# Norm steps in PSUM, four plain blocks at layer 1's second gated half, and three reorderings in a two-layer decoder trunk

## The chip, the cores and the metric

The kernel runs on one core of a Trainium2 chip. The metric is the device time of one execution in microseconds. The kernel before takes 2494.81 us, the median of three runs (2493.42 to 2498.12).

## What is computed

The reference runs a two-layer trunk over a prompt of 1024 tokens and 64 sample tokens (8 sequences of 8), with 1024 channels, in fp32. Every layer is a token mixer and a gated channel mixer, each with an RMS norm ahead and a residual add behind.

```python
def trunk(x, ...):
    h = x
    for layer in range(DEPTH):                       # 2
        hn = rms_norm(h, norm_mix_g[layer])
        if layer % 2 == 0:
            mix = conformer_sb_mixer(hn, ...)        # conv of width 31 | stick-breaking attention, paged cache
        else:
            mix = shortconv_pool_mixer(hn, ...)      # conv of width 3 | pooling of widths 2, 4, 8, 16
        h = h + mix
        h = h + swiglu(rms_norm(h, norm_ffn_g[layer]), w_ffn_in[layer], w_ffn_out[layer])
    return rms_norm(h, norm_final_g)

def rms_norm(x, g):
    return x * rsqrt(mean(x * x) + EPS) * g

def swiglu(h, w_in, w_out):                          # 1024 -> 2 x 2816 -> 1024
    g, u = split(h @ w_in, 2)
    return (silu(g) * u) @ w_out
```

For the sample tokens the keys and values of eight cache pages of 128 tokens per sequence are read through a page table. The outputs are the trunk's rows, the new keys and values and the new states.

## The kernel before

The 1088 tokens are two groups: GA, the first 512 tokens, and GB, the other 576 (512 of the prompt, 64 of the sample). Channels lie on the 128 partitions in eight tiles, tokens in the free dimension; `hb` holds the residual stream that way in SBUF.

Every fp32 product is three matmuls on fp32r operands: high by high, high by low, low by high. So each weight tile of 128x1024 (`stage`, loaded by SyncE's queue) is cut into a high part by ScalarE (L187, or L199 for halves) and a low part by GpSimd (L189, L200), into one of three tiles `hl`. Activations are cut the same way: a high copy on ScalarE, a low part (source minus high) on VectorE or GpSimd. The function `w_next` gives the next weight tile and lets the cuts of the tiles three ahead be issued.

A gated pair (one 128-column slice of gate and one of up) is made in one of two forms. The plain form (`one`) is two blocks of 8 x 3 matmuls over the group's token blocks. The other (`strassen`) takes seven products of half operands in place of eight: it needs sums of weight halves, which VectorE makes (L203 to L205, L217) and ScalarE and GpSimd cut, and sums of operand halves, which are made once per group (`sums_t`, L1743) and cut (`lows`, L1739). `PLAIN1` says how many of the 22 pairs of layer 1 are plain: none for GA, one for GB. A strassen pair of GB has 7 x 4 x 3 = 84 matmuls of 288 columns, a plain one 2 x 8 x 3 x 2 = 96.

A norm is made in these steps. The squares of the eight channel tiles are taken by ScalarE (L251, L254), and seven of the eight are added up into `ss` by GpSimd (L255). TensorE sums `ss` over the partitions, one matmul of one column for each 128 tokens (L262), into a PSUM tile `m`. ScalarE takes the square root (L267), and VectorE refines it in five small steps (L268 to L273), which pass through the SBUF tiles `nw` and `rstd`. VectorE then spreads the result on diagonals (L279), and TensorE (L288) and ScalarE (L289) bring it to `rr`, a row scale for all partitions.

The order of the work on each engine is the order in which the program issues it. The main flow is TensorE's matmuls, and at points between them, called slots, one piece of other work is issued: a step of a generator, or an entry of a list. The places that the change touches are these.

- The sample stage (`sample`, layer 0, beside GA's channel mixer): the attention of the sample tokens. Its last part multiplies weights with value pages, two pages of each of two sequences at a time (`pv`), as pages arrive; `pvq` holds these pieces.
- Layer 1's output of the mixer, GB's part: eight blocks. In their slots the generator `forms_a` makes GA's operands for the strassen products: the normed halves into `fa`, their sums into `fb`, the copies and the low parts. Behind each block `out_fin` adds to `hb` and issues the squares.
- Layer 1's channel mixer for GA (`channel1(GA, ...)`): 22 strassen pairs, with a piece of the output projection behind each pair from the third on. In its slots the generator `forms_b` makes GB's norm and its normed operands `xs`.
- The seam: behind the last pair `free_a` fills the list `seam`, which is worked off in the slots of the output's last pieces (`out_both`). It makes GB's plain operands `b1`, `b2` and, at the end, a part in a `hid` tile. Each of the four jobs of `jobs` makes sums of one quarter of `xs` and cuts them to the strassen operands in `xa`. Two jobs are part of `seam`; the other two are issued at every third slot of GB's plain pair.
- Then GB's channel mixer with the 22 pairs and the final norm.

Of the kernel before, what the change touches and what calls it, by code (L numbers as in the profile page):

```python
# [8 lines left out]
F = mybir.dt.float32  # L9
# [48 lines left out]
def trunk_kernel(ctx, tc, x_prompt, x_sample, cache_k, cache_v, state_conformer, state_shortconv, state_pool,  # L58
# [34 lines left out]
    rstd = consts.tile([128, 9], F, name="rstd")  # L93
    nw = consts.tile([128, 2, 9], F, name="nw")
    hb = hpool.tile([128, KC, T], F, name="hb")
# [43 lines left out]

    PLAIN, PLAIN1 = 5, (0, 1)  # L140

# [115 lines left out]

    def norm_cols(ps, count, t0, t1, more=None):
        m = ps()
        c = slice(t0, t1)  # L260
        for t in range(t0, t1):
            pe.matmul(m[:, t:t + 1], ss[:, t * 128:t * 128 + 128], ones[:, 0:1], start=True, stop=more is None)  # L262
            if more is not None:
                pe.matmul(m[:, t:t + 1], more[:, (t - t0) * 128:(t - t0) * 128 + 128], ones[:, 0:1], start=False,
                          stop=True)
        r = rstd[:, c]
        act.activation(r, m[:, c], AF.Sqrt, bias=eps, scale=1.0 / count)  # L267
        dve.tensor_scalar(nw[:, 0, c], m[:, c], 1.0 / count, EPS, op0=OP.mult, op1=OP.add)  # L268
        dve.reciprocal(r, r)

        dve.tensor_tensor(nw[:, 1, c], nw[:, 0, c], r, op=OP.mult)
        dve.scalar_tensor_tensor(nw[:, 1, c], nw[:, 1, c], -0.5, r, op0=OP.mult, op1=OP.mult)
        dve.scalar_tensor_tensor(r, nw[:, 1, c], 1.5, r, op0=OP.add, op1=OP.mult)  # L273

    def norm_a(g, ps, count, dg=None):
        norm_cols(ps, count, g.t0, g.t1)
        k = g.t1 - g.t0
        dg = tmp() if dg is None else dg
        dve.tensor_tensor(dg[:, :k * 128].rearrange("p (t n) -> p t n", t=k),  # L279
                          ident[:, None, :].to_broadcast([128, k, 128]),  # L280
                          rstd[:, g.t0:g.t1, None].to_broadcast([128, k, 128]), op=OP.mult)
        return dg
# [808 lines left out]
    def sample():  # L1091
# [5 lines left out]
        with ExitStack() as es_:  # L1097
# [192 lines left out]
            while s < len(steps) or chain or pvq or fins:  # L1290
# [6 lines left out]
                if s + 1 < len(steps):  # L1297
                    trans(*steps[s + 1], 0)
                if pvq and not soon and (s % 2 or s >= len(steps)):
                    pvq.pop(0)()  # L1300
                if todo and s < len(steps):
# [429 lines left out]
    def out_fin(g, n, a):  # L1731
        added(g, hb[:, n, g.cs], a)
        add_squares(g, hb[:, n, g.cs], n == 0)

# [16 lines left out]
    def forms_a(ep):  # L1751
        for _ in range(3):
            yield 1
        dg = norm_a(GA, ms, D, ep.tile([128, 1024], F, name="fa"))
        for _ in range(4):
            yield 1
        norm_b(GA, ms, dg)
        yield 1
        w = HALF // 2
        for k in range(4):  # L1760
            fa, fb = (ep.tile([128, 1024], F, name=n) for n in ("fa", "fb"))
            normed(fa[:, :HALF], k, GA.cs)
            normed(fa[:, HALF:], k + 4, GA.cs)
            dsts = ((b1[k][:, :, :w], fa[:, :w]), (b2[k][:, :, :HALF], fa[:, HALF:]),
                    (xa[k][:, :, :HALF], fb[:, :HALF]), (xa[4 + k][:, :, :HALF], fb[:, HALF:]))
            for o, i in dsts[:2]:
                act.activation(o[:, 0], i, AF.Copy)
            yield 1
            b11, b12, b21, b22, t2, t1, t4, t3 = (t[:, i * w:i * w + w] for t in (fa, fb) for i in range(4))
            sums_t(b11, b12, b21, b22, t1, t2, t3, t4)  # L1770
            for o, i in dsts[2:]:
                act.activation(o[:, 0], i, AF.Copy)
            for o, i in dsts[:2]:
                lows(o, i)
            yield 1
            for o, i in dsts[2:]:
                lows(o, i)
            yield 1
# [41 lines left out]


    def forms_b():
        dg = norm_a(GB, ms, D, xs[3])
        yield 1
        yield 1
        norm_b(GB, ms, dg)
        yield 1
        for k in range(4):
            normed(xs[k][:, 0:GB.n], k + 4, GB.cs)
            yield 1  # L1830
            normed(xs[k][:, GB.n:], k, GB.cs)
            yield 1
# [5 lines left out]
    def free_a():  # L1838
# [16 lines left out]
        def job(k):  # L1855
            low()
            b21, b22, b11, b12 = parts_b(k)
            fast = k < 2
            t3 = b12 if k > 1 else fp.tile([128, W2], F, name="t3", bufs=2)
            sums_t(b11, b12, b21, b22, b11, b22, t3, b21)  # L1860
            for o, x in ((xa[k], xs[k][:, W2:3 * W2]), (xa[4 + k][:, :, R], t3), (xa[4 + k][:, :, L], b21)):
                act.activation(o[:, 0], x, AF.Copy)
                if fast:
                    lowq.append(lambda o=o, x=x: lows(o, x))
                else:
                    lows(o, x)

        jobs.extend(lambda k=k: job(k) for k in range(4))
        seam.extend(jobs.pop(0) for _ in range(2))
        rest_b["f"] = last_part  # L1870
# [11 lines left out]
    def channel1(g, last, side, free, plain, x):  # L1882
# [4 lines left out]
        def slot():  # L1887
# [3 lines left out]
            if jobs and g is GB:  # L1891
                if turn[0] % 3 == 0:
                    jobs.pop(0)()
            elif turn[0] % 3 == 0:
                if g is GA or wj[0] > j0 + 2 * plain + 2:
                    next(side, 0)
# [48 lines left out]
    def to_y(hh):  # L1945
# [53 lines left out]
        def finish():  # L1999
            norm_cols(ms, D, 6, 9, last7)  # L2000
            for t in range(6, 9):
# [63 lines left out]
```

## Time and profile before

| | |
|---|---|
| median of three runs | 2494.81 us (2493.42 to 2498.12) |
| the profiled execution's own time | 2494.09 us |
| its span, first to last instruction | 2492.3 us |
| TensorE busy | 2415.4 us (97%) |
| VectorE, GpSimd, ScalarE busy | 1625.9, 1617.5, 1104.3 us |
| mean granted TensorE clock | 0.996 |

In the profile PE is TensorE, PEld its weight loads, DVE VectorE, ACT ScalarE, POOL GpSimd, and L262 line 262 of the kernel before. A row in order of time has the start and the length in us, the engine, line and operation, what is written from what, the shape and how many instructions were merged; in square brackets stand the idle time of the engine ahead of it and what ended that. A merged row's length reaches to the modelled end of its last matmul; the next row's start tells when TensorE went on. A row of the view of waits has the total, the number and the longest. A fp32 matmul that is not split stands as two instructions.

### The profile page before, as it was taken

The page shows a single profiled execution, that of the slowest core. Times are in us where ns is not written, and L with a number is a line of the kernel's source. Part 1 is how long each engine was busy: PE and PEld are TensorE (multiplying, and loading weights), DVE is VectorE, ACT ScalarE, POOL GpSimd, SP SyncE. Part 2 cuts the span into 40 slices and gives each one's busy share as a digit, 9 for nine tenths or more (in the row PEclk, how much of TensorE's full clock was granted, in tenths as well). Part 3 has the DMA queues.
Part 4 walks back from the last instruction along what each step waited for, and adds up shares of the span by engine and source line. Part 5 has one row for each costly group of instructions (what it writes and reads, how often), then busy time and mean ns, then how long its engine had stood idle before and what let it go on. Part 6 is the DMA issues. An engine that isn't in the chain of part 4 may idle for free.

```text
span 2492.3 us, 41476 instructions
## 1 busy us (share of the span) xinstructions
PE 2415.4 (97%) x15877; PEld 2188.2 (88%) x15877; DVE 1625.9 (65%) x2288; ACT 1104.3 (44%) x1877; POOL 1617.5 (65%) x1264
## 2 busy tenths in 40 slices
PE   8999999999999999999999999998999999999998
PEld 6788977788777679999999999888889988999998
DVE  3696878977777553766566533457666668666655
ACT  5535877754444343443333422234343344443333
POOL 6664344655554576787787523277888886887775
PEclk9999999999999999999999999999999999999999
DMA  7332241234665524223232311252333332233322
GB/s 224 113 109 75 76 123 43 72 111 137 179 181 169 161 90 152 77 69 100 87 98 85 113 52 43 61 150 62 92 102 102 100 96 85 85 102 113 92 85 81
DMA packets 355486, 258.32 MB, mean 104 GB/s; under 512 B 22913, under 2 KB 303617, under 8 KB 355272
## 3 DMA queue, kind: packets, MB, share of 16 engines
q1 hardware_dynamic: 355256, 255.66, 34.7%
q8 instruction: 126, 2.06, 0.3%
q14 instruction: 72, 0.59, 0.1%
q10 hardware_dynamic: 32, 0.01, 0.0%
HBM read 237.41 MB, written 18.69 MB: 103 GB/s over the span
## 4 chain that ended last, share of the span: by engine, by line
PE 75%; DVE 13%; POOL 5%; ACT 4%; issue 3%; DMA 1%; SPq 0%; DVEq 0%; ACTq 0%; POOLq 0%
PE acc L238 44%; PE acc L540 22%; POOL hl L200 2%; DVE q L1035 1%; DVE hb L300 1%; PE o L1057 1%; PE m L1159 1%; PE z L1182 1%; PE m L1047 1%; DVE cacc L858 1%; PE z L1018 1%; POOL hl L189 1%; DVE be L1037 1%; DVE sum L203 1%; DVE hid L244 1%
## 5 line engine op out<-in xcount | busy, mean ns | idle before, releaser
L189 POOL TENSOR_TENSOR hl<-stage,hl 128x512 fp32r<-128x512 f32 x464 | 638.6, 1400 | 391.6 <-ACT hl L187 279.9
L238 PE MATMUL acc<-x,hl 128*128 128x512 f32 (+1 forms) x3648 | 771.2, 349 | 11.3 <-DVE tmp L296 3.0
L238 PEld LDWEIGHTS acc<-x,hl 128*128 128x128 f32 x3648 | 585.6, 189 | 74.9 <-issue 5.8
L238 PE MATMUL acc<-hid,hl 128*128 128x288 f32 (+1 forms) x3096 | 542.1, 331 | 5.3 <-DVE hb L300 2.1
L238 PEld LDWEIGHTS acc<-hid,hl 128*128 128x128 f32 x3096 | 468.3, 189 | 51.0 <-DVE hb L300 4.2
L540 PE MATMUL acc<-x,hl 128*128 128x288 f32 (+1 forms) x2676 | 367.9, 291 | 7.9 <-POOL hl L200 3.7
L300 DVE TENSOR_TENSOR hb<-acc,hb 128x512 f32<-128x512 f32 (+1 forms) x360 | 255.5, 718 | 169.9 <-PE acc L238 168.6
L540 PEld LDWEIGHTS acc<-x,hl 128*128 128x128 f32 x2676 | 352.2, 189 | 14.1 <-POOL hl L200 7.0
L200 POOL TENSOR_TENSOR hl<-sum,hl 128x512 fp32r<-128x512 f32 x180 | 234.2, 1331 | 170.1 <-ACT hl L199 168.0
L187 ACT ACTIVATE hl<-stage 128x1024 fp32r<-128x1024 f32 x232 | 243.6, 1054 | 207.7 <-PE acc L238 141.4
L544 DVE TENSOR_TENSOR tmp<-acc,tmp 128x288 f32<-128x288 f32 (+1 forms) x420 | 174.4, 441 | 207.5 <-ACT tmp L556 102.1
L200 POOL TENSOR_TENSOR hl<-stage,hl 128x512 fp32r<-128x512 f32 x180 | 272.4, 1532 | 12.8 <-ACT hl L199 12.8
L540 PE MATMUL acc<-b,hl 128*128 128x256 f32 (+1 forms) x1548 | 216.0, 290 | 7.9 <-DVE tmp L544 5.8
L238 PE MATMUL acc<-x1t,hl 128*128 128x288 f32 x1152 | 216.3, 296 | 1.5 <-POOL hl L189 1.5
L540 PEld LDWEIGHTS acc<-b,hl 128*128 128x128 f32 x1548 | 201.7, 189 | 13.3 <-POOL hl L200 6.7
L238 PEld LDWEIGHTS acc<-x1t,hl 128*128 128x128 f32 x1152 | 195.9, 188 | 19.5 <-POOL hl L189 1.7
L199 ACT ACTIVATE hl<-sum 128x512 fp32r<-128x512 f32 x180 | 103.0, 623 | 187.5 <-DVE sum L205 164.6
L296 DVE TENSOR_TENSOR tmp<-acc,rr 128x512 f32<-128x512 f32 (+1 forms) x108 | 75.1, 710 | 128.1 <-PE acc L238 114.6
L199 ACT ACTIVATE hl<-stage 128x512 fp32r<-128x512 f32 x180 | 105.7, 619 | 70.4 <-PE acc L238 65.5
L507 POOL TENSOR_TENSOR tmp<-tmp 128x576 f32<-128x576 f32 (+1 forms) x85 | 124.3, 1462 | 9.2 <-ACT tmp L484 8.2
L238 PE MATMUL acc<-x1a,hl 128*128 128x512 f32 x480 | 122.6, 410 | 2.5 <-POOL hl L189 1.4
L255 POOL TENSOR_TENSOR ss<-ss,tmp 128x512 f32<-128x512 f32 (+1 forms) x69 | 106.3, 1541 | 25.9 <-ACT tmp L254 15.4
(299 smaller groups left out, 3129.6 us busy)
## 6 DMA issues: line engine op xcount, KB each, us to landing
stage<-in_w_ffn_in_dram SPq DMA_DIRECT2D x176, 512.0 KB
stage<-in_w_ffn_out_dram SPq DMA_DIRECT2D x88, 512.0 KB
stage<-in_w_in_even_dram SPq DMA_DIRECT2D x40, 512.0 KB
kst<-in_cache_k_dram SPq DMA_DIRECT2D x64, 256.0 KB
vst<-in_cache_v_dram SPq DMA_DIRECT2D x56, 256.0 KB
stage<-in_w_out_even_dram SPq DMA_DIRECT2D x16, 512.0 KB
stage<-in_w_in_odd_dram SPq DMA_DIRECT2D x16, 512.0 KB
stage<-in_w_out_odd_dram SPq DMA_DIRECT2D x16, 512.0 KB
```

The source lines that it names most:

```text
L187: act.activation(hl[:, 0], st, AF.Copy)
L189: pool.tensor_tensor(hl[:, 1, c], st[:, c], f32(hl[:, 0, c]), op=OP.subtract)
L199: act.activation(hl[:, 0, c], x, AF.Copy)
L200: pool.tensor_tensor(hl[:, 1, c], x, f32(hl[:, 0, c]), op=OP.subtract)
L203: todo = [lambda: dve.tensor_tensor(sb, su[:, lo], su[:, hi], op=OP.add), lambda: dve.tensor_tensor(sa[:, hi], sg[:, lo], su[:, lo], op=OP ...
L238: pe.matmul(acc[:, b, :c1 - c0], w, xs[:, xi, c0 - o:c1 - o], start=first and s == 0, stop=last and s == 2)
L255: pool.tensor_tensor(ss[:, g.cs], ss[:, g.cs], t[:, :g.n], op=OP.add)
L296: dve.tensor_tensor(d, a, r, op=OP.mult)
L300: dve.tensor_tensor(d, a, d, op=OP.add)
L507: (dve if both and f == NF - 1 else pool).tensor_tensor(t[:, :n], t[:, :n], u[:, :n], op=OP.mult)
L540: pe.matmul(acc[:, :w2], h[:, wi, i, k], xk[:, xi], start=k == 0 and s == 0, stop=k == 3 and s == 2)
L544: dve.tensor_tensor(out, acc[:, :w2], x, op=OP.add)
```

## The change

It has these parts.

1. The small norm steps no longer use `nw` in SBUF: they write other columns of the PSUM tile `m`, and where diagonals follow, the result stays there too.
2. For GB's norm in layer 1 the squares of channel tiles 4 to 7 are no longer added to `ss` by GpSimd. ScalarE writes them to the tiles `xs` (`square`), in the first four slots of GA's channel mixer, GpSimd clears 64 columns of each, and TensorE sums them with `ss`: five one-column matmuls for each 128 tokens. This norm is split into two pieces and stands later.
3. `forms_a` issues copies and low parts one slot behind the step that makes their source.
4. `PLAIN1` is (0, 2): pair 1 of GB is plain too. The first two jobs leave `seam`, and all four are issued at every third slot of the two plain pairs.
5. In the sample stage two slots pass ahead of the last `pv` piece.

At the start of GA's products GpSimd's order was, from the last weight tile of the mixer's output on (`ss` are the sums of squares, `hl` weight cuts; a number tells the pairs' sums apart):

```order
L189 TENSOR_TENSOR hl<-stage,hl 128x512 x2
L255 TENSOR_TENSOR ss<-ss,tmp 128x576
L200 TENSOR_TENSOR hl<-sum_17595,hl 128x512 x2
L255 TENSOR_TENSOR ss<-ss,tmp 128x576
L200 TENSOR_TENSOR hl<-sum_17596,hl 128x512
L200 TENSOR_TENSOR hl<-stage,hl 128x512
L255 TENSOR_TENSOR ss<-ss,tmp 128x576
L200 TENSOR_TENSOR hl<-stage,hl 128x512 x2
L255 TENSOR_TENSOR ss<-ss,tmp 128x576
L200 TENSOR_TENSOR hl<-sum_c,hl 128x512
```

and now it is:

```order
L188 TENSOR_TENSOR hl<-stage,hl 128x512 x2
L199 TENSOR_TENSOR hl<-sum_17589,hl 128x512 x2
L199 TENSOR_TENSOR hl<-sum_17590,hl 128x512
L199 TENSOR_TENSOR hl<-stage,hl 128x512 x3
L1836 MEMSET xs_17729 128x64
L199 TENSOR_TENSOR hl<-sum_c,hl 128x512
```

The four sums between the cuts are gone, and four small memsets have come in, of which the first is shown.

At the end of the sample stage TensorE's order was (`o` are the value products, `vst` and `kst` the pages, `vnew` the new values, `acc<-x` a block of GA's channel mixer):

```order
L1254 MATMUL o<-vst,wts 32x256 x4
L238 MATMUL acc<-x_2_73,hl 128x512 x3
L238 MATMUL acc<-x_3_74,hl 128x512 x3
L1254 MATMUL o<-vst,wts 32x256 x4
L1254 MATMUL o<-kst,wts 32x256 x4
L1261 MATMUL o<-vnew,wts 32x256 x4
```

and now it is:

```order
L1262 MATMUL o<-vst,wts 32x256 x4
L237 MATMUL acc<-x_2_73,hl 128x512 x3
L237 MATMUL acc<-x_3_74,hl 128x512 x3
L237 MATMUL acc<-x_4_75,hl 128x512 x3
L237 MATMUL acc<-x_5_76,hl 128x512 x3
L237 MATMUL acc<-x_6_77,hl 128x512 x3
L237 MATMUL acc<-x_7_78,hl 128x512 x3
L1262 MATMUL o<-vst,wts 32x256 x4
L1262 MATMUL o<-kst,wts 32x256 x4
L1269 MATMUL o<-vnew,wts 32x256 x4
```

Four groups of three matmuls have moved ahead of the last two pages.

At the seam VectorE's order, from the last plain operand on, was (`xs` and `t` are the sums of the first job, `x_` its low parts, `hb<-acc` the adds that free an accumulator of the output):

```order
L1739 TENSOR_TENSOR b_3_16851<-xs_17745,b_3_16851 128x288
L1743 TENSOR_TENSOR xs_17742<-xs_17742 128x288
L1743 TENSOR_TENSOR t_21464<-xs_17742 128x288
L1743 TENSOR_TENSOR xs_17742<-xs_17742 128x288 x2
L1739 TENSOR_TENSOR x_0_71<-xs_17742,x_0_71 128x576
L300 TENSOR_TENSOR hb<-acc,hb 128x512
L1739 TENSOR_TENSOR x_4_75<-t_21464,x_4_75 128x288
L1739 TENSOR_TENSOR x_4_75<-xs_17742,x_4_75 128x288
```

and now it is:

```order
L1751 TENSOR_TENSOR b_3_16850<-xs_17732,b_3_16850 128x288
L308 TENSOR_TENSOR hb<-acc,hb 128x512 x4
L1751 TENSOR_TENSOR hid<-xs_17729,hid 128x288
L1751 TENSOR_TENSOR hid<-xs_17730,hid 128x288
L1751 TENSOR_TENSOR hid<-xs_17731,hid 128x288
L1751 TENSOR_TENSOR hid<-xs_17732,hid 128x288
L1755 TENSOR_TENSOR xs_17729<-xs_17729 128x288
L1755 TENSOR_TENSOR t_21579<-xs_17729 128x288
```

The adds and the last plain part come first, and the first job follows them.

The diff, with the renamed arguments of the last norm and the removed tile `nw` left out:

```diff
@@ -137,7 +136,7 @@
             add_out(w_ffn_out[l], NF // 2 - 1, o)
-    PLAIN, PLAIN1 = 5, (0, 1)
+    PLAIN, PLAIN1 = 5, (0, 2)
     EVEN = [(j, c) for c in range(4) for j in (0, 1, 2, 3)] + [(4, c) for c in range(4)]
@@ -255,30 +254,39 @@
         pool.tensor_tensor(ss[:, g.cs], ss[:, g.cs], t[:, :g.n], op=OP.add)
-    def norm_cols(ps, count, t0, t1, more=None):
+    def norm_cols(ps, count, t0, t1, more=()):
+        m = norm_sums(ps, count, t0, t1, more)
+        norm_rest(m, count, t0, t1, rstd[:, t0:t1])
+
+    def norm_sums(ps, count, t0, t1, more=()):
         m = ps()
+        for t in range(t0, t1):
+            cs = [ss[:, t * 128:t * 128 + 128]] + [q[:, (t - t0) * 128:(t - t0) * 128 + 128] for q in more]
+            for i, q in enumerate(cs):
+                pe.matmul(m[:, t:t + 1], q, ones[:, 0:1], start=i == 0, stop=i == len(cs) - 1)
+        act.activation(rstd[:, t0:t1], m[:, t0:t1], AF.Sqrt, bias=eps, scale=1.0 / count)
+        return m
+
+    def norm_rest(m, count, t0, t1, out):
         c = slice(t0, t1)
-        for t in range(t0, t1):
-            pe.matmul(m[:, t:t + 1], ss[:, t * 128:t * 128 + 128], ones[:, 0:1], start=True, stop=more is None)
-            if more is not None:
-                pe.matmul(m[:, t:t + 1], more[:, (t - t0) * 128:(t - t0) * 128 + 128], ones[:, 0:1], start=False,
-                          stop=True)
-        r = rstd[:, c]
-        act.activation(r, m[:, c], AF.Sqrt, bias=eps, scale=1.0 / count)
-        dve.tensor_scalar(nw[:, 0, c], m[:, c], 1.0 / count, EPS, op0=OP.mult, op1=OP.add)
+        a, b, r = m[:, 16 + t0:16 + t1], m[:, 32 + t0:32 + t1], rstd[:, c]
+        dve.tensor_scalar(a, m[:, c], 1.0 / count, EPS, op0=OP.mult, op1=OP.add)
         dve.reciprocal(r, r)
-        dve.tensor_tensor(nw[:, 1, c], nw[:, 0, c], r, op=OP.mult)
-        dve.scalar_tensor_tensor(nw[:, 1, c], nw[:, 1, c], -0.5, r, op0=OP.mult, op1=OP.mult)
-        dve.scalar_tensor_tensor(r, nw[:, 1, c], 1.5, r, op0=OP.add, op1=OP.mult)
+        dve.tensor_tensor(b, a, r, op=OP.mult)
+        dve.scalar_tensor_tensor(b, b, -0.5, r, op0=OP.mult, op1=OP.mult)
+        dve.scalar_tensor_tensor(out, b, 1.5, r, op0=OP.add, op1=OP.mult)
     def norm_a(g, ps, count, dg=None):
-        norm_cols(ps, count, g.t0, g.t1)
+        return norm_diag(g, norm_sums(ps, count, g.t0, g.t1), count, tmp() if dg is None else dg)
+
+    def norm_diag(g, m, count, dg):
         k = g.t1 - g.t0
-        dg = tmp() if dg is None else dg
+        r = m[:, 48 + g.t0:48 + g.t1]
+        norm_rest(m, count, g.t0, g.t1, r)
         dve.tensor_tensor(dg[:, :k * 128].rearrange("p (t n) -> p t n", t=k),
                           ident[:, None, :].to_broadcast([128, k, 128]),
-                          rstd[:, g.t0:g.t1, None].to_broadcast([128, k, 128]), op=OP.mult)
+                          r[:, :, None].to_broadcast([128, k, 128]), op=OP.mult)
         return dg
     def spread(g, ps, src, scale):
@@ -1297,6 +1305,9 @@
                 if s + 1 < len(steps):
                     trans(*steps[s + 1], 0)
                 if pvq and not soon and (s % 2 or s >= len(steps)):
+                    if nv[0] == 32 and len(pvq) == 1:
+                        yield 1
+                        yield 1
                     pvq.pop(0)()
                 if todo and s < len(steps):
                     yield 1
@@ -1730,7 +1741,8 @@
     def out_fin(g, n, a):
         added(g, hb[:, n, g.cs], a)
-        add_squares(g, hb[:, n, g.cs], n == 0)
+        if g is GA or n < 4:
+            add_squares(g, hb[:, n, g.cs], n == 0)
     def normed(out, c, cs, view=lambda ap: ap):
         dve.scalar_tensor_tensor(out, view(hb[:, c, cs]), pc(FFNG + 8 + c), view(rr[:, cs]), op0=OP.mult, op1=OP.mult)
@@ -1763,15 +1775,16 @@
             normed(fa[:, HALF:], k + 4, GA.cs)
             dsts = ((b1[k][:, :, :w], fa[:, :w]), (b2[k][:, :, :HALF], fa[:, HALF:]),
                     (xa[k][:, :, :HALF], fb[:, :HALF]), (xa[4 + k][:, :, :HALF], fb[:, HALF:]))
+            yield 1
+            b11, b12, b21, b22, t2, t1, t4, t3 = (t[:, i * w:i * w + w] for t in (fa, fb) for i in range(4))
+            sums_t(b11, b12, b21, b22, t1, t2, t3, t4)
             for o, i in dsts[:2]:
                 act.activation(o[:, 0], i, AF.Copy)
             yield 1
-            b11, b12, b21, b22, t2, t1, t4, t3 = (t[:, i * w:i * w + w] for t in (fa, fb) for i in range(4))
-            sums_t(b11, b12, b21, b22, t1, t2, t3, t4)
+            for o, i in dsts[:2]:
+                lows(o, i)
             for o, i in dsts[2:]:
                 act.activation(o[:, 0], i, AF.Copy)
-            for o, i in dsts[:2]:
-                lows(o, i)
             yield 1
             for o, i in dsts[2:]:
                 lows(o, i)
@@ -1819,9 +1832,16 @@
     seam, jobs, rest_b = [], [], {}
+    def square(k):
+        pool.memset(xs[k][:, GB.n:640], 0.0)
+        act.activation(xs[k][:, 0:GB.n], hb[:, 4 + k, GB.cs], AF.Square)
+
+    ahead1 = [lambda k=k: square(k) for k in range(4)]
+
     def forms_b():
-        dg = norm_a(GB, ms, D, xs[3])
+        m = norm_sums(ms, D, GB.t0, GB.t1, xs)
         yield 1
+        dg = norm_diag(GB, m, D, xs[3])
         yield 1
         norm_b(GB, ms, dg)
         yield 1
@@ -1855,18 +1875,13 @@
         def job(k):
             low()
             b21, b22, b11, b12 = parts_b(k)
-            fast = k < 2
             t3 = b12 if k > 1 else fp.tile([128, W2], F, name="t3", bufs=2)
             sums_t(b11, b12, b21, b22, b11, b22, t3, b21)
             for o, x in ((xa[k], xs[k][:, W2:3 * W2]), (xa[4 + k][:, :, R], t3), (xa[4 + k][:, :, L], b21)):
                 act.activation(o[:, 0], x, AF.Copy)
-                if fast:
-                    lowq.append(lambda o=o, x=x: lows(o, x))
-                else:
-                    lows(o, x)
+                lows(o, x)
         jobs.extend(lambda k=k: job(k) for k in range(4))
-        seam.extend(jobs.pop(0) for _ in range(2))
         rest_b["f"] = last_part
     def go_on():
@@ -1891,6 +1906,8 @@
             if jobs and g is GB:
                 if turn[0] % 3 == 0:
                     jobs.pop(0)()
+            elif ahead1:
+                ahead1.pop(0)()
             elif turn[0] % 3 == 0:
                 if g is GA or wj[0] > j0 + 2 * plain + 2:
                     next(side, 0)
```

More of the change, by code (lines that the diff above doesn't have):

```diff
@@ L93, in trunk_kernel @@
     rstd = consts.tile([128, 9], F, name="rstd")
-    nw = consts.tile([128, 2, 9], F, name="nw")
     hb = hpool.tile([128, KC, T], F, name="hb")
@@ L1999, in finish @@
         def finish():
-            norm_cols(ms, D, 6, 9, last7)
+            norm_cols(ms, D, 6, 9, [last7])
             for t in range(6, 9):
```

## The prediction

> **What bounds the kernel now.** I read the page first, then who waits for whom on TensorE stage by stage, then the rows in order of time at the places the change touches.
>
> ```profile
> PE 2415.4 (97%) x15877; PEld 2188.2 (88%) x15877; DVE 1625.9 (65%) x2288; ACT 1104.3 (44%) x1877; POOL 1617.5 (65%) x1264
> ```
>
> TensorE works almost without a break: the span of 2492.3 us holds 76.9 us in which it is idle. So a microsecond is won only where a wait of TensorE goes away, and each added matmul costs its full length. Three places of the change hold waits, and the views of waits for these stretches (total, times, longest) name them. First the sample stage's end (855 to 905 us), then the start of layer 1's gated products for the first row group (1690 to 1740), then the seam to the second group (2030 to 2110):
>
> ```profile
> PE o L1254 <- DMA kst<-in_cache_v_dram: 1.6, 1, 1.6
> ...
> PE acc L540 <- POOL hl L200: 2.9, 3, 1.7
> PE acc L540 <- DVE tmp L544: 2.7, 1, 2.7
> PE acc L238 <- POOL hl L189: 1.5, 1, 1.5
> ...
> PE acc L540 <- DVE tmp L544: 2.3, 1, 2.3
> PE acc L238 <- DVE hb L300: 1.8, 1, 1.8
> PE acc L540 <- ACT x L1862: 1.3, 1, 1.3
> ...
> PE acc L540 <- DVE x L1739: 0.4, 1, 0.4
> ```
>
> The change addresses 1.6, then 7.1 (2.9 + 2.7 + 1.5), then 3.5 (1.8 + 1.3 + 0.4). The 2.3 belongs to the first group's last two products, which it leaves alone.
>
> **Sample end.** TensorE's rows around the last two value pages:
>
> ```profile
> 854.80 1.07 PE L1254 MATMUL o<-kst,wts 128*32 128x256 f32 x16
> 855.80 1.67 PE L238 MATMUL acc<-x,hl 128*128 128x512 f32 x6
> ...
> 860.00 0.64 PE L1254 MATMUL o<-vst,wts 128*32 128x256 f32 x8
> ...
> 863.00 0.41 PE L1254 MATMUL o<-kst,wts 128*32 128x256 f32 x2 [1.60 <-DMA kst<-in_cache_v_dram]
> ...
> 863.99 1.66 PE L238 MATMUL acc<-x,hl 128*128 128x512 f32 x6
> ```
>
> From 860.00 to 863.99 pass 3.99 us. Sixteen such matmuls take 1.00 (854.80 to 855.80), and the eight of vnew behind them are half as many: 1.5 us of work, so 2.5 lost, of which 1.60 stand as the wait for the page's transfer. Two slots are four groups of three matmuls with 512 columns. Six of these take 1.6 at most (855.80's row), so the last pages are asked for up to 3 us later, at about 862.8, and the second of them at 863.4, when it has landed (863.00). Its issue is not moved: the pair ahead, which frees the buffer, stands where it stood. Queued behind the moved pieces are the last head fill and the second norm of the convolution, which follow two slots later; the hand over to the next stage comes long after. **-2.4.** Bounds: 0 if the transfer slips too, -2.5.
>
> **First group's seam.** VectorE's and GpSimd's rows there:
>
> ```profile
> 1701.49 1.88 POOL L255 TENSOR_TENSOR ss<-ss,tmp 128x576 f32<-128x576 f32 x1
> ...
> 1709.68 1.30 POOL L200 TENSOR_TENSOR hl<-sum,hl 128x512 fp32r<-128x512 f32 x1
> ...
> 1717.41 1.42 POOL L255 TENSOR_TENSOR ss<-ss,tmp 128x576 f32<-128x576 f32 x1
> ...
> 1726.81 1.22 DVE L272 SCALAR_TENSOR_TENSOR nw<-nw,rstd 128x5 f32<-128x5 f32 x1
> ...
> 1729.31 1.88 DVE L279 TENSOR_TENSOR xs<-ident,rstd 128x640 f32<-128x640 f32 x1
> ```
>
> Four sums of squares stand between the weight cuts (hl) that the 2.9 us are waited for; the first and the last are shown, 1.88 and 1.42, and all four are 6.6 us of GpSimd that go; four small memsets come. The last three norm steps and the diagonal hold VectorE from 1726.8 to 1731.2 (1729.31 + 1.88), and the sums and accumulator reads behind them come late: that is the 2.7. They move behind the third product. The 1.5 is ScalarE's: its weight copy stood behind copies that waited 4.52 for fa:
>
> ```profile
> 1694.41 0.42 ACT L1767 ACTIVATE b<-fa 128x256 fp32r<-128x256 f32 x1 [4.52 <-DVE fa L1736]
> ...
> 1697.14 1.04 ACT L187 ACTIVATE hl<-stage 128x1024 fp32r<-128x1024 f32 x1
> ```
>
> In the new order that weight copy stands ahead of these copies. What the stretch could take without waits comes from the chain's rows (start, us) in the same loop's steady part, and TensorE's rows in order of time give what it took:
>
> ```profile
> 1842.81 2.90 PE acc L540 x22
> 1845.71 5.60 PE acc L238 x24
> ...
> 1858.86 2.90 PE acc L540 x22
> ...
> 1701.59 6.13 PE L238 MATMUL acc<-x1t,hl 128*128 128x288 f32 x44 [1.51 <-POOL hl L189]
> ...
> 1724.23 1.17 PE L262 MATMUL m<-ones,ss 128*128 128x1 f32 x10
> 1725.26 1.67 PE L540 MATMUL acc<-x,hl 128*128 128x256 f32 x12
> ...
> 1733.93 2.41 PE L540 MATMUL acc<-b,hl 128*128 128x256 f32 x12 [2.74 <-DVE tmp L544]
> ...
> 1746.93 4.36 PE L238 MATMUL acc<-hid,hl 128*128 128x512 f32 x18
> ```
>
> A product and a quarter of the output take 16.05 (1842.81 to 1858.86), so a product alone 16.05 - 5.60 = 10.45. From 1700.08 (1701.59 less its wait) to 1746.93 are 46.85 us, for a block of 6.0, three products (31.35) and the norm's columns (1.03): 38.4. The loss is 8.5. How much comes back? Three products without an output piece follow each other, and the 2.3 at the end of this loop shows that two alone already wait once for VectorE. With 6.6 us of GpSimd and 4.4 of VectorE gone I leave 1.5: **-7.0**. Bounds: -8.5, and -3.9 if each of the second and third products waits that 2.3.
>
> **The price there.** The sums of squares of n = 4 to 7 are no longer added up by GpSimd but by TensorE: 25 one-column matmuls in place of 5. The row at 1724.23 counts 10 instructions for 5, and they take 1.03 (to 1725.26). So 40 more instructions, **+4.1**, on the engine that sets the end; bounds +4.1, and +2 if TensorE would have waited for weight cuts right there. The squares stay four ScalarE instructions of the same size. The diagonal and its spread come one output piece later, and so do the eight normed pieces: those have the whole loop, some 300 us.
>
> **Second group's seam.** The 1.8 stands because VectorE does the first two operand jobs between the accumulator adds of the output; now these jobs follow it. The 1.3 and 0.4 are the first product waiting for jobs three and four:
>
> ```profile
> 2069.39 0.44 DVE L1743 TENSOR_TENSOR xs<-xs 128x288 f32<-128x288 f32 x1
> ...
> 2072.86 4.48 PE L238 MATMUL acc<-hid,hl 128*128 128x512 f32 x18 [1.85 <-DVE hb L300]
> ...
> 2083.11 3.99 DVE L1743 TENSOR_TENSOR xs<-xs 128x288 f32<-128x288 f32 x4
> 2087.01 1.48 DVE L1739 TENSOR_TENSOR x<-xs,x 128x576 fp32r<-128x576 f32 x3
> 2088.42 3.86 DVE L1743 TENSOR_TENSOR xs<-xs 128x288 f32<-128x288 f32 x4
> 2092.55 1.50 DVE L1739 TENSOR_TENSOR x<-xs,x 128x576 fp32r<-128x576 f32 x3 [0.26 <-ACT x L1862]
> ```
>
> A job took 5.4 us there (2083.11 to 2094.0 for two). Four plain blocks now cover four jobs: at 48 matmuls each, 4 x 6.4 = 25.5 us, against 4 x 5.4 = 21.7 and some 5 us of other VectorE work between them (an estimate: a gate product, three weight sums and five low parts, at 0.4 to 0.8 each by the width of their rows). That is about even, and the last operand is needed a little into the product, so I leave 0.5 of the 3.5: **-3.0**; bounds -3.5 and, with the jobs late, +3 (below). The price: a plain pair is 96 matmuls, a product 84, at the same 288 columns:
>
> ```profile
> 1128.45 12.77 PE acc L238 x96
> ...
> 2225.53 11.19 PE acc L540 x84
> ```
>
> 12.77 - 11.19 = **+1.6**. GpSimd has four cuts where the product had seven, DMA loads the same two tiles.
>
> **Norm steps elsewhere: 0.** Eleven other places do the same steps, and where GpSimd is idle each lasts 0.17 already:
>
> ```profile
> 41.61 0.17 DVE L272 SCALAR_TENSOR_TENSOR nw<-nw,rstd 128x4 f32<-128x4 f32 x1
> ```
>
> Only at the end of the program does TensorE not cover them:
>
> ```profile
> 2484.71 0.16 DVE L268 TENSOR_SCALAR nw<-m 128x3 f32<-128x3 f32 x1 [1.28 <-ACT rstd L267]
> ```
>
> A step that reads PSUM, this one, is as short, so 0, bounds -1 and +0.5.
>
> The sum: -2.4 - 7.0 + 4.1 - 3.0 + 1.6 = -6.7. The profiled execution took 2494.09, so 2487.4; the median of the runs shown is 0.7 above it: **2488**.
>
> **A rule against part of it.** Behind the 2.74 us gap TensorE's granted clock was 0.83 over ten microseconds, which is 3.4 us at half speed, and the twelve matmuls at 1733.93 took 2.41 where others take 1.67: 0.8 of the 8.5.
>
> ```profile
> 1730.00:1740.00 10.00, 7.26 (x48) 7.08 (x48) 7.68 (x13) 5.66 (x9) 6.71 (x6) 0.83 0.18 51
> ```
>
> The Trainium skill, "TensorE: Matmul & The Clock Gate", section "HAM oscillation", lets the clock drop only behind a gap above some 3.4 us. By that rule the slow matmuls would not go with this gap and the time would be 0.8 higher; the trace has the drop behind 2.74, so it disagrees.
>
> **The rivals.** *The limit only moves* (chance 0.25). GpSimd's cuts for three products in a row, 21 halves and two gates, are 30 us at the 1.30 of the row at 1709.68, and more where VectorE reads beside them, against TensorE's 31.35: no slack. If the second and third products each wait 2.3, the seam returns 3.9, 3.1 less than forecast: 2491. With one more wait at the moved norm, where ScalarE's square root holds the weight copies behind it until the 25 matmuls are done, 2493. For it speaks the 2.3; against it that the sums now start some 3 us earlier.
>
> *The operand jobs overrun the four plain blocks* (0.10): slower than before. Plain blocks bring GpSimd's cuts back to back with the jobs, whose sums read two SBUF tiles; four sums took 3.99 at 2083.11, and at 2069.39, with GpSimd idle, 4 x 0.44 = 1.8. If all four jobs take 5.7 (3.99 + 1.48 + 0.26) and the 5 us of other work nearly double to 9, VectorE needs 32 us from the output's end; TensorE asks for the last operand 25.5 + 1.2 after it (a quarter of two half products on). From there each microsecond is a wait: up to 5, and a half-speed window of 1.7. Then the seam costs 5 + 1.7 + 1.6 - 1.8 = +6.5 instead of -1.4, and the sum is +1.2: 2496. The Trainium skill, "SBUF — State Buffer", section "Who interferes with whom", says that a VectorE instruction with two SBUF inputs contends with a GpSimd one that reads SBUF; by that rule, which the 1.22 against 0.17 above bears out, PSUM norm steps escape it and the jobs do not.
>
> *The norm's columns are free* (0.10): TensorE would have waited for cuts there anyhow, and the loss of 8.5 returns whole: -2.4 - 8.5 + 2 - 3.5 + 1.6 = -10.8, 2484.
>
> **How the numbers follow.** The forecast has 0.55, its own range 2485 to 2491. The range of 2483 to 2495 leaves out a part of the last two rivals. Faster by over 0.2% (5 us, about what a measurement of this kernel can tell from no change) means under 2489.8: most of the forecast and the free columns, 0.57. Within: the rest of the forecast, the moved limit and most of the overrun, 0.35. Slower: 0.08.
>
> **What would show it.** Right: no wait for kst at the end of the sample stage; no GpSimd wait on the block before the products; 50 rows of L266 between third product and output, 5.2 us long; no hb wait in the output; 96 more matmuls in plain form. Wrong: L552 waits of 2 us and more in the first three products, or a wait of the second group's first product for x, and half clock behind either.

## The result, and the profile after

The changed kernel takes 2479.27 us (median of 6 runs, 2477.03 to 2481.64), the kernel before 2495.49 us beside it: a ratio of 0.9938, with a 95% interval of 0.9927 to 0.9948. It is 16.2 us faster where the forecast's sum was 6.7, and 2479 lies below the range of 2483 to 2495. The profiled execution took 2479.13 us, with a span of 2477.4. Ratios leave out one execution of the kernel called nw kept below, which took 4748 us.

The waits of TensorE in the three stretches that the change addresses (engine, operation and line, what was waited for, then total, times and longest in us): the sample stage's end, the start of layer 1's gated products for the first group, the seam to the second group.

```profile
PE acc L237 <- DVE hb L308: 1.7, 1, 1.7
PE acc L237 <- POOL hid L243: 1.1, 1, 1.1
...
PE acc L548 <- POOL hl L199: 1.1, 1, 1.1
PE acc L548 <- DVE tmp L552: 0.6, 1, 0.6
...
PE acc L548 <- DVE tmp L552: 2.3, 1, 2.3
PE acc L237 <- DVE hid L243: 0.7, 1, 0.7
```

The wait for the page (1.6) is gone, the first group's 7.1 are 1.7, and of the second seam's 3.5 nothing is left. So the edits do to the waits what was forecast, with one exception: behind the sample stage stand 1.7 and 1.1 where before stood 0.9.

TensorE's rows at the first group's seam (start, us, line, operation, count, wait ahead):

```profile
1714.85 2.30 PE L548 MATMUL acc<-b,hl 128*128 128x256 f32 x14
1718.26 1.46 PE L548 MATMUL acc<-b,hl 128*128 128x256 f32 x10 [1.11 <-POOL hl L199]
...
1728.94 1.67 PE L548 MATMUL acc<-b,hl 128*128 128x256 f32 x12 [0.62 <-DVE tmp L552]
1730.45 0.28 PE L266 MATMUL m<-ones,ss 128*128 128x1 f32 x2
...
1736.31 8.59 PE L237 MATMUL acc<-hid,hl 128*128 128x512 f32 x24
1744.73 4.47 PE L548 MATMUL acc<-x,hl 128*128 128x256 f32 x36
...
1755.77 5.73 PE L237 MATMUL acc<-hid,hl 128*128 128x512 f32 x24
```

The norm's columns take from 1730.45 to 1736.31, 5.86 us, and the output piece behind them 8.59 where the next one takes 5.73. The second is the clock's doing, as the windows show (the granted clock is the last number but two):

```profile
1720.00:1730.00 10.00, 9.38 (x79) 9.21 (x78) 4.43 (x8) 5.25 (x9) 10.00 (x9) 1.00 0.32 94
1730.00:1736.00 6.00, 6.00 (x55) 6.00 (x53) 3.79 (x7) 2.71 (x4) 3.36 (x4) 0.96 0.35 109
1736.00:1746.00 10.00, 10.00 (x38) 8.22 (x38) 3.70 (x10) 2.59 (x6) 5.15 (x5) 0.68 0.01 2
```

None of this explains some 9 us more than forecast. Those come from stretches that the change does not touch. Matmuls of the first group's last gated pair in layer 0 and of its output, after (runs of 78 and 52) and then before (the same in runs of 90 and 96, since the order ahead of them differs):

```profile
898.31 17.98 PE L237 MATMUL acc<-x,hl 128*128 128x512 f32 x78
916.12 11.95 PE L237 MATMUL acc<-hid,hl 128*128 128x512 f32 x52
```

```profile
900.86 21.33 PE L238 MATMUL acc<-x,hl 128*128 128x512 f32 x90
922.03 22.65 PE L238 MATMUL acc<-hid,hl 128*128 128x512 f32 x96
```

From start to start, 916.12 - 898.31 = 17.81 us for 78 is 228.3 ns a matmul; before, 21.17 for 90 is 235.2. Nothing waits in these rows, and the instructions are the same. Taken over all pairs of neighbouring matmuls that both traces have, without waits and without half clock, such small differences (up to 20 ns a pair) add up to some -16 us.

### The profile page after: what moved, and what is told of

It is laid out like the page before. It is cut to its first block, busy times and chain, and to the rows that moved or that the text cites. A ratio compares the mean times of both kernels' runs of the same rounds, so it can differ in the third digit from the quotient of the medians.

```text
span 2477.4 us, 41551 instructions
## 1 busy us (share of the span) xinstructions
PE 2407.3 (97%) x15929; PEld 2194.3 (89%) x15929; DVE 1613.3 (65%) x2278; ACT 1102.1 (44%) x1871; POOL 1607.2 (65%) x1260
## 4 chain that ended last, share of the span: by engine, by line
PE 53%; DVE 5%; POOL 3%; issue 1%; ACT 0%; DVEq 0%; ACTq 0%; POOLq 0%
PE acc L237 29%; PE acc L548 22%; POOL hl L199 2%; DVE hid L243 1%; DVE fa L1748 0%; PE m L266 0%; PE blk L1979 0%; DVE sum L202 0%; DVE sum L203 0%; POOL tmp L515 0%; DVE sum L204 0%; DVE hb L308 0%; DVE x L1751 0%; DVE tmp L552 0%; DVE x L243 0%
## 5 line engine op out<-in xcount | busy, mean ns | idle before, releaser
L548 PE MATMUL acc<-x,hl 128*128 128x288 f32 (+1 forms) x2628 | 358.6, 291 | 3.5 <-DVE tmp L552 2.4
L548 PE MATMUL acc<-b,hl 128*128 128x256 f32 (+1 forms) x1512 | 210.8, 290 | 5.3 <-DVE tmp L552 3.3
L515 POOL TENSOR_TENSOR tmp<-tmp 128x512 f32<-128x512 f32 (+1 forms) x84 | 122.1, 1454 | 9.2 <-ACT tmp L492 8.2
L243 DVE TENSOR_TENSOR hid<-tmp,hid 128x576 fp32r<-128x576 f32 (+1 forms) x66 | 79.5, 1206 | 64.1 <-ACT hid L242 64.1
```

Source lines behind the costliest of these rows:

```text
L243: (on or dve).tensor_tensor(dst[:, 1], src, f32(dst[:, 0]), op=OP.subtract)
L515: (dve if both and f == NF - 1 else pool).tensor_tensor(t[:, :n], t[:, :n], u[:, :n], op=OP.mult)
L548: pe.matmul(acc[:, :w2], h[:, wi, i, k], xk[:, xi], start=k == 0 and s == 0, stop=k == 3 and s == 2)
```

## The experiments

All ratios are against the kernel before, run beside it on the same chip. Where two variants are compared, the difference of their ratios is taken of 2495 us; by the intervals of the two ratios such a difference is good to some 4 to 6 us.

**Is it the tile that went?** The norm steps in PSUM leave the tile `nw` without use, and the change drops it. It took 72 bytes of a partition, 96 with rounding, near the bottom of SBUF's left side. In the compiled program all that lies behind it stands 96 bytes lower: the weight tiles `hl` at 44768 and not 44864, `hb`, the operands `b` and `tt`. The right side (`x1`, `x1a`, `x1t`, the other `hid`) stays.

```diff
     rstd = consts.tile([128, 9], F, name="rstd")
+    pad = consts.tile([128, 2, 9], F, name="pad")      # a_nw_kept; [128, 8]: a_pad32; [128, 16]: a_pad64
```

> The changed kernel with a tile of nw's size (72 bytes a partition) kept, unused, at nw's old place; no instruction differs. Theory (placement): dropping nw moved every tile behind it on the left side of SBUF down by 96 bytes (hl from 44864 to 44768), and that alone makes TensorE's matmuls of 512 and 288 columns up to 2% quicker, some 10 us of the 16; the edits give the rest. Then this run takes 2488 to 2490 us. Rival (edits): the 16 us come from the edits alone, the tile's place is nothing: 2479 (2477 to 2482).

> The changed kernel with an unused tile of 32 bytes a partition at nw's old place: the left side moves up by 32, hl to 44800, a multiple of 64 as before the change. Placement with a period of 64 bytes: 2488 to 2490, as with nw kept. Placement by some longer period: anything from 2478 to 2490. Edits alone: 2479.

> The changed kernel with an unused tile of 64 bytes a partition at nw's old place: hl at 44832, 32 bytes off a multiple of 64 as in the changed kernel. Placement with a period of 64 bytes: 2479, as the changed kernel. Placement by a longer period: anything from 2478 to 2490. Edits alone: 2479.

> The kernel before with an unused tile of 32 bytes a partition behind nw, nothing else: hl at 44896, 32 bytes off a multiple of 64. Placement with a period of 64 bytes: some 10 us less than before, 2484 to 2486. Edits alone: 2495, no change.

Measured: nw kept 2491.86 (0.9993, 0.9983 to 1.0003); 32 bytes 2489.77 (0.9982, 0.9973 to 0.9992); 64 bytes 2486.04 (0.9968, 0.9956 to 0.9979); the kernel before with 32 bytes more 2492.00 (0.9992, 0.9982 to 1.0001). An unused tile in the old place takes nearly the whole gain away: in that place the edits alone are not to be told from no change. The placement theory stands, its period of 64 bytes does not: 64 bytes cost 7.5 us, and the kernel before gains only some 2. The rows of the 78 matmuls with nw kept:

```profile
900.52 18.52 PE L238 MATMUL acc<-x,hl 128*128 128x512 f32 x78
918.88 12.34 PE L238 MATMUL acc<-hid,hl 128*128 128x512 f32 x52
```

18.36 us for 78 is 235.4 ns, as before. The two kernels, which differ in the edits and not in the place, also agree matmul by matmul: small differences, counted as above, add up to 0.2 us over the run.

**The norm steps alone, and the place alone.**

```diff
-    nw = consts.tile([128, 2, 9], F, name="nw")
...
-        dve.tensor_scalar(nw[:, 0, c], m[:, c], 1.0 / count, EPS, op0=OP.mult, op1=OP.add)
+        dve.tensor_scalar(wa, m[:, c], 1.0 / count, EPS, op0=OP.mult, op1=OP.add)     # b_psum: wa, wb in m
```

> The kernel before with the norm steps in PSUM and the nw tile gone, and no other part of the change: orders, sums of squares, sample stage and seams as before. The forecast had 0 for this part (bounds -1 and +0.5): 2494 to 2495. Placement: the left side of SBUF stands where it stands in the changed kernel, 96 bytes lower, so the matmuls of 512 columns step at 227 ns in place of 234 and this part alone takes some 12 us off: 2481 to 2484.

```diff
-    rstd = consts.tile([128, 9], F, name="rstd")
-    nw = consts.tile([128, 2, 9], F, name="nw")
+    small = consts.tile([128, 30], F, name="rstd")     # b_one_tile: also holds eps and brow
+    rstd, eps = small[:, 0:9], small[:, 9:10]
+    nw = small[:, 12:30].rearrange("p (a b) -> p a b", a=2)
```

> The kernel before with rstd, eps, brow and nw as parts of one tile, which puts every tile behind them on the left side 96 bytes lower, where the changed kernel has them (hl 44768); the norm steps stay in SBUF and no instruction is added or gone. If the distance alone is what the norm steps in PSUM brought: 2484 to 2486, as the kernel before with PSUM steps (2484.7). If steps in PSUM are quicker by themselves: 2490 to 2495.

Measured: steps in PSUM alone 2484.69 (0.9958, 0.9944 to 0.9972), one tile and steps in SBUF 2484.74 (0.9961, 0.9947 to 0.9975). The second adds no instruction and moves only tiles, and gains the same 10 us. So the steps in PSUM are worth nothing measurable by themselves; the place is worth it all. The rows of the version with one tile:

```profile
902.06 20.67 PE L238 MATMUL acc<-x,hl 128*128 128x512 f32 x90
922.57 11.95 PE L238 MATMUL acc<-hid,hl 128*128 128x512 f32 x52
```

20.51 us for 90 is 227.9 ns, where the kernel before has 235.2. Against these two, which have the changed kernel's place, the rest of the change gains 5.0 and 5.7 us.

**Whose place?** First the right side was moved under a left side that stayed, then the left side behind `hl`.

```diff
+    padr = ctx.enter_context(tc.tile_pool(name="padr", bufs=1, side="right")).tile([128, 8], F, name="padr")
     x1p = x1stack.enter_context(tc.tile_pool(name="x1b", bufs=1, side="right"))          # a_right32
...
+    padh = hpool.tile([128, 8], F, name="padh")        # a_behind32
     hb = hpool.tile([128, KC, T], F, name="hb")
```

> The changed kernel with an unused tile of 32 bytes at the outer end of SBUF's right side: every tile of the right side (x1, x1a, x1t, tmp, the first hid) 32 bytes lower, the left side (hl, hb) as in the changed kernel. If the distance between the operand on the right and the weights on the left decides, it is as with 32 bytes put in on the left: the step of 232 and 235 ns in turn for the 512 columns, 2489 to 2491. If the left side's own address decides: 227 ns, 2479. If any shift does harm by chance: something else.

> The changed kernel with an unused tile of 32 bytes behind the weight buffers on the left side: hl stays at 44768, hb and all that follows on the left (b1, b2, tt, the second hid) stands 32 bytes higher. If the distance between hl and the operand decides: x, x1a and the first hid on the right keep their steps (227 ns at 512 columns), and only matmuls with left operands (b, tt, hid of the first layer's second group) may change, some 3700 matmuls by up to 2 ns: 2475 to 2485. If the place of hb and the tiles behind it decides: 2488 to 2491, as with 32 bytes ahead of hl.

Measured: right side 32 lower 2488.45 (0.9976, 0.9966 to 0.9987); tiles behind `hl` 32 higher 2483.09 (0.9958, 0.9941 to 0.9974). The 78 and 52 matmuls, with the right side moved and then with the tiles behind `hl` moved:

```profile
898.77 18.45 PE L238 MATMUL acc<-x,hl 128*128 128x512 f32 x78
917.05 12.29 PE L238 MATMUL acc<-hid,hl 128*128 128x512 f32 x52
```

```profile
897.28 17.98 PE L238 MATMUL acc<-x,hl 128*128 128x512 f32 x78
915.09 11.95 PE L238 MATMUL acc<-hid,hl 128*128 128x512 f32 x52
```

With the right side moved, 18.28 us for 78 (234.4 ns), the same as with 32 bytes put in on the left (18.28 there too): for these operands it is the distance between the two, and neither address by itself. With only the tiles behind `hl` moved, these operands keep their 17.81. There, left operands change: `b` at 256 columns and `tt`, which kept their time under the other moves (groups by line and shape: busy us, mean ns), after and then with the tiles behind `hl` moved:

```profile
L548 PE MATMUL acc<-tt,hl 128*128 128x288 f32 x816 | 113.6, 295 | 0.0
L548 PE MATMUL acc<-b,hl 128*128 128x256 f32 x792 | 107.6, 285 | 4.2 <-DVE tmp L552 2.9 <-POOL hl L199 1.1
```

```profile
L549 PE MATMUL acc<-tt,hl 128*128 128x288 f32 x816 | 114.2, 295 | 0.0
L549 PE MATMUL acc<-b,hl 128*128 128x256 f32 x792 | 106.5, 283 | 4.3 <-DVE tmp L553 3.0 <-POOL hl L200 1.1
```

One thing does not fit a rule of two addresses: with the tiles behind `hl` moved, layer 1's last output pieces take 12.78 us where they took 12.48, though their `hid` (on the right) and `hl` stand where they stood. They follow products with `b`, which did move. The output pieces of layer 0's second group, which have the same size, take 12.80 and 12.48 in turn in the changed kernel, and 12.80 each time under either of these two moves. What a stretch is worth seems to depend also on how the matmuls ahead of it leave the engine; that is open. So the distance is shown for the products with 512 columns on the right side, and not for every product.

**The price of the columns.** Two ways to have the norm with 5 columns again: the four squares added up by GpSimd as before the change, or by VectorE, one add a slot behind the first products.

```diff
-        m = norm_sums(ms, D, GB.t0, GB.t1, xs)
+        for k in range(4):                             # a_dve_adds
+            dve.tensor_tensor(ss[:, GB.cs], ss[:, GB.cs], xs[k][:, 0:GB.n], op=OP.add)
+            yield 1
+        m = norm_sums(ms, D, GB.t0, GB.t1)
```

> The changed kernel with the four squares of n = 4 to 7 added up by GpSimd again, as before the change, so the norm has 5 one-column matmuls and not 25; the other parts stay. By the forecast's terms the waits for the weight cuts come back (2.9 to 5.5 us) and 4.1 us of columns go: 2478 to 2480. If the columns also drop TensorE's clock (half speed for 6.8 us there in the changed kernel), 2 to 3.4 us more go: 2475 to 2477.

> The changed kernel with the four squares added to ss by VectorE, one a slot behind the first three products, and the norm's 5 columns behind them, one or two output pieces later; the memsets go. By the forecast's price for the columns alone: 4.1 us less, 2475. If the columns also drop the clock: 2471 to 2473. If VectorE's adds make its reads of the accumulators late in the same stretch: 2477 to 2480.

Measured: GpSimd 2477.28 (0.9931, 0.9915 to 0.9948), not told apart from the changed kernel; VectorE 2471.82 (0.9912, 0.9896 to 0.9929), 6.5 us faster than it. Waits with GpSimd's sums, then with VectorE's adds, and the windows of the latter at the seam:

```profile
PE acc L548 <- POOL hl L199: 4.5, 5, 1.6
```

```profile
PE acc L548 <- POOL hl L199: 1.6, 2, 1.0
```

```profile
1719.00:1729.00 10.00, 9.38 (x79) 9.21 (x78) 4.43 (x8) 5.25 (x9) 10.00 (x8) 1.00 0.32 101
1729.00:1736.00 7.00, 6.68 (x34) 5.21 (x33) 7.00 (x12) 3.03 (x6) 4.36 (x4) 1.00 0.27 83
1736.00:1746.00 10.00, 9.46 (x77) 9.05 (x77) 5.71 (x10) 3.33 (x6) 10.00 (x8) 1.00 0.25 63
```

GpSimd's adds bring 3.4 us of waits back (4.5 for 1.1), VectorE's 0.5. Without the 20 columns the clock stays at 1.00 there. All eight kernels with the 25 columns show half speed at this place, for 3.4 to 10.2 us; the four on the changed order with 5 show none. So by the waits taking the sums off GpSimd was right (the two ways differ by 4.7 us, which is about the error of the difference), and TensorE was the wrong engine to give them to. VectorE's version is 22 us faster than the kernel before.

**More distances.** On the version with VectorE's adds, the left side was lowered further, by putting eps and brow into other small tiles.

> The version with VectorE's adds (2471.8), eps put into the first column of one tile with brow, so that the left side stands another 32 bytes lower (hl 44736) and the distance to the right side is 32 bytes less; no instruction is added or gone. Theory that the distance decides and the changed kernel's happens to be a good one: the step of the 512 columns leaves 227 ns and the time rises by 7 to 13, to 2479 to 2485, as for the three distances tried above it. Rival, every step down is a gain: under 2471.

> The same version with eps and brow both put into rstd's tile: 64 bytes lower than the changed kernel (hl 44704). Theory: 7 to 13 us above 2471.8, or 227 ns and 2471.8 again if good distances come back every so often. Rival, every step down is a gain: under 2470.

Measured: 32 lower 2485.15 (0.9960, 0.9945 to 0.9975), 64 lower 2476.64 (0.9928, 0.9912 to 0.9943). Lower on the left is farther from the right side, not nearer as the first of these expectations has it. Of the seven distances tried the changed kernel's gives the shortest step. By the same matmuls: 234.4 ns at 32 lower, 230.1 at 64 lower, 228.3 here, 234.4 at 32 and at 64 higher, 235.4 at 96 and 233.2 at 128 (the kernel before with 32 bytes more). Odd multiples of 32 cost 10 to 14 us. Even ones cost 4 to 8, of which the 4 (64 lower) is within the error and fits neither expected case, so only the odd step down surely loses. The step at 512 columns is not all of it: it is 234.4 with 32 and with 64 bytes more, and the second is 3.5 us quicker. Its 256-column products of `x` step at 116.0 on average, against 118.4.

**The two other edits, undone one at a time on the changed kernel.**

```diff
-    PLAIN, PLAIN1 = 5, (0, 2)
+    PLAIN, PLAIN1 = 5, (0, 1)                          # a_seam2_old, with
+        seam.extend(jobs.pop(0) for _ in range(2))
...
-                    if nv[0] == 32 and len(pvq) == 1:  # a_sample_old
-                        yield 1
-                        yield 1
```

> The changed kernel with layer 1's second seam as before: two plain blocks for the second group, the first two operand jobs between the output's adds. Placement is that of the changed kernel. The forecast gave -3.0 for the waits and +1.6 for the matmuls, so undone it is 1.4 slower: 2480.5 to 2481. If the jobs overran the four plain blocks, it would be faster, 2473 to 2478.

> The changed kernel without the two slots of delay for the last value pages. The forecast gave -2.4: 2481.7 undone. By the traces of the two kernels of one placement, in which the stretch behind the sample stage came 1.0 to 1.65 earlier: 2480.3 to 2481. Unmoved at 2479.3 if the wait was hidden by what follows.

Measured: second seam undone 2484.08 (0.9951, 0.9938 to 0.9965), 3 us slower; sample delay undone 2480.60 (0.9944, 0.9930 to 0.9957), 1.5 us slower. Neither is told from nothing by the times alone. Without the seam's edit the three waits stand again (2.2, 1.4 and 0.4):

```profile
PE acc L237 <- DVE hb L308: 2.2, 1, 2.2
PE acc L548 <- ACT x L1882: 1.4, 1, 1.4
```

## Why the prediction missed

The kernel with nw kept has the place of the kernel before, so that the two traces show the edits alone. The starts of the same matmuls, with nw kept and then before:

```profile
943.66 0.51 PE L238 MATMUL acc<-x,hl 128*128 128x288 f32 x2 [1.64 <-DVE hb L309]
...
1704.17 4.42 PE L549 MATMUL acc<-x,hl 128*128 128x256 f32 x36
...
1737.38 0.28 PE L267 MATMUL m<-ones,ss 128*128 128x1 f32 x2
...
1745.59 7.94 PE L238 MATMUL acc<-hid,hl 128*128 128x512 f32 x24
1753.36 4.39 PE L549 MATMUL acc<-x,hl 128*128 128x256 f32 x36
...
2051.79 4.60 PE L238 MATMUL acc<-hid,hl 128*128 128x512 f32 x19
```

```profile
945.55 0.63 PE L238 MATMUL acc<-x,hl 128*128 128x288 f32 x3 [0.88 <-DVE hb L300]
...
1707.56 3.21 PE L540 MATMUL acc<-x,hl 128*128 128x256 f32 x26
...
1753.61 4.39 PE L540 MATMUL acc<-x,hl 128*128 128x256 f32 x36
...
2051.20 5.70 PE L238 MATMUL acc<-hid,hl 128*128 128x512 f32 x22
```

In the chain of waits the product that stood at 2225.53 stands here:

```profile
2223.34 11.19 PE acc L549 x84
```

They come earlier by 1.89, 3.39 and 0.25, then later by 0.59, and behind the second seam earlier by 2.19. The end does so by 1.8 (spans of 2490.5 and 2492.3), and by the ratio it is 1.7, give or take 2.5, where the forecast had 6.7.

- **Sample end, -2.4: the wait went, the gain only in part.** With the place held it is 1.7, the 1.89 less 0.2 that stood there at 838 us already. What failed there is that the hand over "comes long after": the next wait, for `hb`, grows from 0.88 to 1.64.
- **First group's seam, -7.0: right.** From the first product to the norm pass 33.21 us (1737.38 - 1704.17), for three products without waits of 31.35; before it was 39.37 to the output, 38.34 without the norm's 1.03. With the block's 1.51 that is -6.6, and the waits left are 1.7 where I left 1.5. The rival that the limit only moves did not come: neither 2.3 appears.
- **The norm's columns, +4.1: mis-sized.** They take 8.21 us with nw kept and 5.86 in the changed kernel, not 5.2, and the output piece behind them 7.94 and 8.59 where another takes 5.73. In the changed kernel that is 4.8 (5.86 less 1.03) and 2.9, so 7.7, and with nw kept 7.2 and 2.2, so 9.4; the run with VectorE's adds got 6.5 of it back. What the sum lacked is the half clock; I had put it down to the gap of 2.74 alone and expected it to go with the gap. The Trainium skill, "TensorE: Matmul & The Clock Gate", section "HAM oscillation", has the drop behind a gap of some 3.4 us; here the longest gap ahead of it is 1.11, TensorE is busy for 6.00 of the 6.00 us of the columns, and the clock drops all the same.
- **Second seam, -3.0 and +1.6: right, if anything too small.** With the place held 2.8: the output ahead of the seam starts 0.59 later than before (the spread of the norm, 1.0, now stands between, and half speed fell there: a granted clock of 0.83 from 2036 to 2046), and the product behind it 2.19 earlier. By the run that undoes it 3; the sum had 1.4. The jobs did not overrun.
- **Norm steps elsewhere, 0: the step that failed.** The steps are worth 0, as said, but the term stood for all that goes with them, and the tile that they freed moved the weights. That is some 10 us by two kernels that hold nothing else, and 13.7 between the changed kernel and the one with nw kept; in the traces of these two, quicker matmuls make 17.2, of which longer waits take 5.7 back. I had held that "a microsecond is won only where a wait of TensorE goes away". In a kernel whose TensorE is busy for 97%, the time of the matmuls themselves was the larger term, and no view of the profile lists it as a wait.

The likeliest case was right about the waits. In the old place its sum was too good by some 5 us for the edits (1.7 for 6.7), nearly all of it the columns (9.4 for 4.1), and it lacked the 13.7 that came from the place. In the new place the edits gain 5.0 to 5.7, near the 6.7, and the place some 10; the runs do not tell these two ways of splitting the 16 us apart.

## What to carry to other kernels

Where TensorE is busy nearly all the time, compare the step of the same unwaited matmuls before looking at any wait: a run of 78 in one row each is enough. A small tile added or dropped early in a pool moves every tile behind it, so test an edit with the tile kept (an unused one of its size) before its gain is put down to the edit; and once the order is done, try a few paddings between weights and operands. Sums moved to TensorE as one-column matmuls cost their time and then half clock; four adds on an engine with slack cost less.

## What the runs showed of the hardware that was not expected

- **The distance between weights and moving operand changes the matmul's step**: 228 to 235 ns at 512 columns (3%) over seven distances 32 bytes apart. The steps repeat: neighbouring starts inside such a run are mostly 232 and 235 ns in turn at 32 bytes more (233 and 234 with the right side moved instead), run through a cycle of seven between 231 and 238 at the old distance, and at the changed one are 226 or 227 once the run has settled. At 256 columns the order is the other way: the products of `x` step at 119.7 ns on average at the changed distance (most steps are 120) and at 115.5 to 119.1 at the others. That the reads of the next weights and of the operand meet in SBUF would explain it, but no run shows the cause. The Trainium skill, "SBUF — State Buffer", section "SBUF: two separate sides", gives the weight load a read port of its own and says that TensorE never waits on anyone; taken at its word, the place would not matter, and here it does.
- **One-column matmuls bring the half clock**, behind 5 us of them without a gap (0.96, then 0.68 in the next ten microseconds). A short wait does so only sometimes: every one of the sixteen profiles has a wait of 2.3 us behind the first group's last products, and seven of them show 3.4 us of half speed there.
- **A profiled execution carries some microseconds of chance**: in the changed kernel's a half-speed stretch of 10.2 us stands at 418 us, where the other profiles of the changed order have 3.4 us or none. Times were therefore compared by medians, and traces only inside stretches without it.
